# Scan decays of a hybrid encoder layer: biases inside the exponentials, feature decays broadcast by DMA, time steps by token

## The chip, the cores and the metric

One core of a Trainium2 chip runs the kernel. The metric is device time in microseconds, the median of several runs; lower is better. Engines are named as in the profile: PE is TensorE (matmuls; PEld its weight loads), DVE is VectorE, ACT is ScalarE, POOL is GpSimd, SP is the engine that issues most of the DMAs. Each works through its own list in order and waits for the others by semaphores.

## The reference, cut to what matters

The layer is a mixer of two branches (a bidirectional state space scan and windowed attention), a cross attention and a feed forward part, all in float32, with 512 tokens of 1024 features. The change concerns the scan: 32 heads of 64 features in 4 groups, 4 chunks of 128 tokens, once forward and once backward.

```python
dtf = softplus(dt_f + dt_bias_f); dtb = softplus(dt_b + dt_bias_b)   # (tokens, heads)
af = -exp(a_log_f); ab = -exp(a_log_b)                              # (heads)
def ssd_chunked(xh, dt, a_head, b_in, c_in):
    a_cum = cumsum(dt * a_head)                  # within each chunk of 128 tokens
    x_c = xh * dt
    seg = a_cum[l] - a_cum[s]
    decay = exp(where(lower, seg, -inf))         # per head and chunk, 128 x 128
    cb = einsum('bclgn,bcsgn->bclsg', c_c, b_c)  # per group
    y_diag = einsum('bclsg,bclsgr,bcsgrp->bclgrp', cb, decay, x_c)
    to_end = exp(a_cum[last] - a_cum)
    states = einsum('bclgn,bclgr,bclgrp->bcgrpn', b_c, to_end, x_c)
    chunk_decay = exp(a_cum[last])
    h_in = scan over chunks: state * chunk_decay + states
    y_off = einsum('bclgn,bcgrpn,bclgr->bclgrp', c_c, h_in, exp(a_cum))
    return y_diag + y_off
y = ssd_chunked(forward) + flip(ssd_chunked(backward)) + d_skip * xh
```

## The kernel before, in words

**Weights.** All projections run with features on the partitions and 512 tokens along the free axis. A weight granule of 128x1024 is loaded by SP (line 120) into one of two raw buffers, cast by ACT to a high part (line 128), and DVE (POOL for ten of them) subtracts to get the low part (line 129). A projection is then 24 matmuls of 512 columns, eight each of lines 138, 139 and 140. Granules are loaded and split two ahead of their use.

**Order.** The program is a list of steps, in which scan steps and projections are woven (`weave`, the strings `ONE`, `TWO`, `LAST`). A scheduler of the tile framework turns it into one order for each engine, taking what is ready by its own model of time; it also sets all waits. Tiles rotate: a tile with `bufs=2` may be written again when all readers of the tile two before are done.

**Time steps** (`dt_step`). One granule gives 64 rows (32 heads, two directions) by 512 tokens. Lines 345 to 362 compute the softplus on 64x512: ACT takes exp(-|v|), DVE evaluates a polynomial as seven pairs of a multiplication (line 354) and an addition (line 355), divides (line 349), multiplies by the head's rate (line 361); ACT takes the logarithm (line 363). PE then turns three results to tokens on partitions (`tok`, line 368, four transposes each). Matmuls with triangles give the cumulative sums, by heads (line 380) and by tokens (line 387). The rows by heads are stored to DRAM (`adr`, line 383). `nb` is log(dt) minus the cumulative sum, `wt` and `dec` are the weights of a chunk and its decay. The buffer `x1` is free then and holds what lies between. In program order the first group's convolutions follow (lines 408 to 414: one step of ACT, four of DVE, tanh on ACT, one of DVE, for each of six granules); DVE gets them mixed with the time steps.

**A group's scan** (`group_scan`). `weigh` (POOL, line 492) and `carry` (PE line 500, DVE 505 and 507) compute the states. Each of eight heads then goes through stages: `rows` loads the cumulative sums of both directions, broadcast over 128 partitions, into `rt` (line 516, three buffers); `head` lets ACT write exp of half of the partitions to `ear` (line 528: the decay by features, one tile of two buffers for a pair of heads), POOL mask both directions (line 530), ACT take the exponential of the forward part with `nb` as a bias per partition, chunk by chunk (line 536), DVE add `nb` to the backward part chunk by chunk (line 538) and ACT take the exponential of that as one instruction (line 539). `both` (POOL, line 545) adds the directions into `mt` (three buffers), `times` (DVE, line 550) multiplies by the group's `cb`, `inner` and `arrive` (PE, lines 560 and 572) are the products for a pair of heads. `gather` (lines 580 to 585) multiplies what arrives by `ear` on DVE and adds it on DVE and POOL; `gate` follows. Between the stages the next group's convolutions, the gates `z` and the former group's output projections run. At a group's end, PE turns the last convolution's output to tokens (line 467).

Of the kernel before, what the change touches and what calls it, by code (L numbers as in the profile page):

```python
# [15 lines left out]
P = 128  # L16
# [13 lines left out]
# columns of the packed constants  # L30
# [7 lines left out]
V_DTB, V_AL, V_DSK, V_SNK = 200, 201, 202, 218  # L38
V_N = 234
# granules of the input projection  # L40
# [32 lines left out]
def bidir_hybrid_layer(ctx: ExitStack, tc: tile.TileContext, io, dbg=None):  # L73
# [17 lines left out]
    adr = dram.tile([64, S], F32, tag="adr", name="adr")  # L91

# [94 lines left out]
    def gain_split(hi, lo, t, g):  # L187
        """hi + lo = t * g, exactly split."""
# [26 lines left out]
    # ======================= keys and values of the memory =======================  # L215
    # (in buffers that the state space branch uses later)
# [111 lines left out]
    # ======================= state space branch =======================  # L328
# [7 lines left out]
    # time steps: softplus, cumulative sums within chunks, decays  # L336
    # (x1 is free until the first group is projected: it holds the intermediate values)
    def dt_step(w):
        acc = proj(w, st["hh"], st["hl"])
        v, e, den, s2, pl = (x1[0:64, i] for i in range(5))  # L340

        def t256(i, o):
            return x1[:, i, 256 * o:256 * o + 256].rearrange("p (c e) -> p c e", c=NCH)
# [13 lines left out]
        dt, dta, ld = den, s2, e  # L357
        nc.vector.scalar_tensor_tensor(dt, v, 0.0, pl, op0=ALU.max, op1=ALU.add)
        an = st["sp"].tile([64, 1], F32, tag="an", name="an")
        nc.scalar.activation(an, vec[0:64, V_AL:V_AL + 1], AF.Exp)  # L360
# [860 lines left out]
```

## Time and profile before

| what | value |
|---|---|
| median of 3 runs | 1351.72 us (1351.01 to 1351.82) |
| profiled execution, from first to last instruction | 1350.6 us |
| PE, DVE, ACT, POOL busy | 1284.6, 812.4, 580.8, 316.5 us |
| time steps and first convolutions | 55 to 104 us |
| scan of four groups | 104 to 530 us |
| attention, merge, cross attention, feed forward | 530 us to the end |

Busy time of an engine is the time in which at least one instruction of it runs. Matmuls are pipelined, so PE can be busy without being at its peak. A wait names the instruction that came last among those waited for. The chain of waits is followed back from the last instruction, at each step to what released it, or to the instruction before it on its engine. The granted clock is given as a share of TensorE's full speed, averaged over the stretch.

### The profile page before, as it was taken

To read this page: it belongs to the slowest core of one execution; us is meant where nothing else is said; L and a number is where in the kernel's file an instruction comes from. 1 tells how busy PE (TensorE), PEld (TensorE's weight loads), DVE (VectorE), ACT (ScalarE), POOL (GpSimd) and SP (SyncE) were. 2 spreads that over 40 slices of the span, in tenths; PEclk is the share of its full clock that TensorE was granted. 3 is DMA by queue.
4 is the path that set the end of the run, shared out by engine and by line. 5 is a ranking of instruction groups with operands and counts; after the bars stand their busy time and mean duration, and the time that the engine had idled before them with its cause. 6 is when DMAs were issued, how large, how long until landed. Compare 5 with 4: busy or idle time off the path is not lost.

```text
span 1350.6 us, 16359 instructions
## 1 busy us (share of the span) xinstructions
PE 1284.6 (95%) x6084; PEld 1022.9 (76%) x6084; DVE 812.4 (60%) x1355; ACT 580.8 (43%) x1001; POOL 316.5 (23%) x259
## 2 busy tenths in 40 slices
PE   6889998998999999999999999999999999999996
PEld 5667776776777678876656888888888888888886
DVE  5797788788679776577765444566443444333323
ACT  6437376257256253256855333444332332222221
POOL 3344254234453562320000001100211111110001
PEclk9999999998999999999999999999999999999998
DMA  7435344243223323321102332411323322233331
GB/s 244 129 102 160 112 143 129 74 125 125 69 94 119 109 74 99 115 80 46 47 16 85 118 94 94 156 63 49 101 88 105 96 94 94 96 102 90 99 98 63
DMA packets 45440, 134.95 MB, mean 100 GB/s; under 512 B 5104, under 2 KB 8560, under 8 KB 45360
## 3 DMA queue, kind: packets, MB, share of 16 engines
q1 hardware_dynamic: 43072, 129.77, 30.4%
q10 hardware_dynamic: 1584, 2.03, 0.5%
q0 software_dynamic: 704, 2.10, 0.4%
q8 instruction: 48, 0.79, 0.2%
q14 instruction: 32, 0.26, 0.1%
HBM read 129.55 MB, written 4.33 MB: 99 GB/s over the span
## 4 chain that ended last, share of the span: by engine, by line
PE 69%; DVE 12%; issue 6%; POOL 6%; ACT 4%; DMA 2%; SPq 0%; DVEq 0%; POOLq 0%; ACTq 0%
PE mm L138 19%; PE mm L140 19%; PE mm L139 19%; DVE cvu L411 2%; DVE rt L538 2%; DVE wlo L129 2%; PE sa L774 2%; PE sb L813 2%; PE sb L800 1%; POOL mt L545 1%; POOL vv L585 1%; PE sa L772 1%; PE sb L986 1%; ACT whi L128 1%; PE sb L500 1%
## 5 line engine op out<-in xcount | busy, mean ns | idle before, releaser
L138 PE MATMUL mm<-hh,whi 128*128 128x512 f32 x968 | 388.4, 401 | 8.8 <-DVE cvu L411 5.4
L128 ACT CAST whi<-raw 128x1024 fp32r<-128x1024 f32 (+2 forms) x192 | 199.0, 1037 | 454.4 <-PE mm L139 394.0
L140 PE MATMUL mm<-hh,wlo 128*128 128x512 f32 x968 | 383.5, 397 | 0.9 <-DVE wlo L129 0.8
L139 PE MATMUL mm<-hl,whi 128*128 128x512 f32 x968 | 382.5, 395 | 0.2 <-DVE hl L310 0.2
L129 DVE TENSOR_TENSOR wlo<-raw,whi 128x1024 fp32r<-128x1024 f32 (+2 forms) x193 | 242.4, 1257 | 127.4 <-ACT whi L128 121.1
L138 PEld LDWEIGHTS mm<-hh,whi 128*128 128x128 f32 x968 | 184.8, 191 | 52.1 <-issue 10.3
L140 PEld LDWEIGHTS mm<-hh,wlo 128*128 128x128 f32 x968 | 184.2, 190 | 43.1 <-issue 2.3
L139 PEld LDWEIGHTS mm<-hl,whi 128*128 128x128 f32 x968 | 184.5, 191 | 39.0 <-issue 1.6
L185 POOL TENSOR_TENSOR sq_acc<-sq_acc,sq 128x512 f32<-128x512 f32 x14 | 24.8, 1771 | 276.4 <-ACT sq L184 276.4
L1039 POOL TENSOR_TENSOR fa<-fa,row 128x512 f32<-128x512 f32 x22 | 39.1, 1779 | 192.3 <-ACT fa L1038 192.3
L411 DVE SCALAR_TENSOR_TENSOR cvu<-mm,hcw,cvu 128x510 f32<-128x510 f32 (+1 forms) x96 | 70.9, 739 | 5.9 <-ACT cvu L408 5.5
L138 PE MATMUL mm<-fh,whi 128*128 128x512 f32 (+1 forms) x198 | 72.4, 366 | 0.0
L139 PE MATMUL mm<-fl,whi 128*128 128x512 f32 (+1 forms) x198 | 72.4, 365 | 0.0
L140 PE MATMUL mm<-fh,wlo 128*128 128x512 f32 (+1 forms) x198 | 72.4, 365 | 0.0
L138 PE MATMUL mm<-vh,whi 128*128 128x512 f32 (+1 forms) x192 | 71.5, 373 | 0.0
L140 PE MATMUL mm<-vh,wlo 128*128 128x512 f32 (+1 forms) x192 | 69.3, 361 | 0.0
L139 PE MATMUL mm<-vl,whi 128*128 128x512 f32 (+1 forms) x192 | 68.8, 358 | 0.0
L538 DVE TENSOR_SCALAR rt<-rt,nb 128x128 f32<-128x128 f32 x128 | 52.5, 466 | 20.9 <-POOL rt L530 17.5
L545 POOL TENSOR_TENSOR mt<-rt 128x512 f32<-128x512 f32 x32 | 48.0, 1503 | 71.8 <-ACT rt L539 33.8
L1041 DVE TENSOR_TENSOR ft<-fa,mm 128x512 f32<-128x512 f32 x22 | 15.1, 688 | 72.8 <-PE mm L140 70.7
L528 ACT ACTIVATE ear<-rt 64x1024 f32<-64x1024 f32 x32 | 33.9, 1060 | 55.7 <-POOL vv L585 51.9
L140 PE MATMUL mm<-oh,wlo 128*128 128x512 f32 x128 | 50.2, 392 | 0.0
(233 smaller groups left out, 2070.3 us busy)
## 6 DMA issues: line engine op xcount, KB each, us to landing
raw<-in_w_in SPq DMA_DIRECT2D x69, 512.0 KB, 3.5
raw<-in_w_fi SPq DMA_DIRECT2D x44, 512.0 KB, 3.5
rt<-adr SPq DMA_DIRECT2D x64, 256.0 KB, 4.3
raw<-in_w_bs SPq DMA_DIRECT2D x16, 512.0 KB, 3.4
raw<-in_w_fo SPq DMA_DIRECT2D x16, 512.0 KB, 3.5
raw<-in_w_xk SPq DMA_DIRECT2D x8, 512.0 KB, 3.8
raw<-in_w_ba SPq DMA_DIRECT2D x8, 512.0 KB, 3.4
raw<-in_w_mo SPq DMA_DIRECT2D x8, 512.0 KB, 3.5
```

What stands on the lines that cost most here:

```text
L128: nc.scalar.copy(hi[:, t], raw[:, t])
L129: (nc.gpsimd if i in LO_POOL else nc.vector).tensor_tensor(lo[:, t], raw[:, t], hi[:, t].bitcast(F32), op=ALU.subtract)
L138: nc.tensor.matmul(acc, wh, xh[:, k0 + k], start=first and k == 0, stop=False)
L139: nc.tensor.matmul(acc, wh, xl[:, k0 + k], start=False, stop=False)
L140: nc.tensor.matmul(acc, wl, xh[:, k0 + k], start=False, stop=last and k == nk - 1)
L411: nc.vector.scalar_tensor_tensor(u[:, b], acc[:, a], w5[j], u[:, b], op0=ALU.mult, op1=ALU.add)
L528: nc.scalar.activation(st["ear", h // 2][own], rt[own], AF.Exp)
L538: nc.vector.tensor_scalar(r, r, st["nb"][:, c, e0:e0 + 1], None, op0=ALU.add)
L545: nc.gpsimd.tensor_tensor(mt, st["rt", g, h][:, 0], st["rt", g, h][:, 1], op=ALU.add)
L774: nc.tensor.matmul(sp[:, :n], qs[own, qb * P:(qb + 1) * P], st["kl"][own, pr, b0 * P:b1 * P], start=False, stop=True)
L813: nc.tensor.matmul(av[64 * kk:64 * kk + 64], st["vt"][:, b0 + j, h * 64:(h + 1) * 64], st["pt", kk, j], start=j == 0, stop=j == b1 - b0 - 1)
L1039: nc.gpsimd.tensor_tensor(a, a, st["row2"], op=ALU.mult)
```

## The change

1. The backward part of a head gets its `nb` as a bias of four exponentials, as the forward part did: DVE's additions of line 538 and the single exponential of line 539 go.
2. The exponential of the cumulative sums is taken once for all heads on 64x512 in `dt_step`, stored to DRAM (`edr`) and broadcast by SP into `ear`, two copies of 64 partitions for a pair of heads (`earows`). The first two pairs' copies stand after the heads of steps 2 and 4, the others after the `gather` that frees their buffer. The rows of a head come as one copy of 512 KB in place of two.
3. The time steps are turned to tokens before the softplus, with four transposes, and run on 128x256; multiplications and additions are fused; the logarithm comes last. `V_AL` holds the rates broadcast over the partitions, and the vectors are 297 columns wide in place of 234.

```diff
     def dt_step(w):
         acc = proj(w, st["hh"], st["hl"])
-        v, e, den, s2, pl = (x1[0:64, i] for i in range(5))
-        nc.scalar.activation(v, acc[0:64], AF.Identity, bias=vec[0:64, V_DTB:V_DTB + 1])
-        nc.scalar.activation(e, v, AF.Abs)
+        v, e, den, s2, pl, dta, ld, acm = (slot(i) for i in range(8))
+        raw, rows, erows = (x1[0:64, i] for i in (5, 6, 7))
+        nc.scalar.activation(raw, acc[0:64], AF.Identity, bias=vec[0:64, V_DTB:V_DTB + 1])
+        tp = bank("sb")
+        tpv = tp[:, 0:256].rearrange("p (c e) -> p c e", c=NCH)
+        for c in range(NCH):
+            nc.tensor.transpose(tpv[:, c], raw[:, c * P:(c + 1) * P], ident[0:64, 0:64])
+        an = st["sp"].tile([P, 64], F32, tag="an", name="an")
+        nc.scalar.activation(an, vec[:, V_AL:V_AL + 64], AF.Exp)
+        nc.scalar.activation(e, tpv, AF.Abs)
+        nc.vector.tensor_copy(v, tpv)
         nc.scalar.activation(e, e, AF.Exp, scale=-1.0)
...
-        nc.vector.tensor_scalar(pl, s2, 2.0 / 17.0, 2.0 / 15.0, op0=ALU.mult, op1=ALU.add)
-        for n in (13, 11, 9, 7, 5, 3, 1):
-            nc.vector.tensor_tensor(pl, pl, s2, op=ALU.mult)
-            nc.vector.tensor_scalar(pl, pl, 2.0 / n, None, op0=ALU.add)
-        nc.vector.tensor_tensor(pl, pl, e, op=ALU.mult)
+        nc.vector.tensor_scalar(pl, s2, 2.0 / 17.0, None, op0=ALU.mult)
+        for n in (15, 13, 11, 9, 7, 5, 3):
+            nc.vector.scalar_tensor_tensor(pl, pl, 2.0 / n, s2, op0=ALU.add, op1=ALU.mult)
+        nc.vector.scalar_tensor_tensor(pl, pl, 2.0, e, op0=ALU.add, op1=ALU.mult)
...
-        nc.vector.tensor_scalar(dta, dt, an, -1.0, op0=ALU.mult, op1=ALU.mult)
+        anb = an.rearrange("p (o e) -> p o e", o=1).broadcast_to([P, NCH, 64])
+        nc.vector.scalar_tensor_tensor(dta, dt, -1.0, anb, op0=ALU.mult, op1=ALU.mult)
         nc.vector.tensor_scalar(ld, dt, 1e-37, None, op0=ALU.max)
-        nc.scalar.activation(ld, ld, AF.Ln)
...
-        dat = tok(dta, t256(5, 0))
-        dtt = tok(dt, t256(5, 1))
-        ldt = tok(ld, t256(7, 1))
...
-        nc.scalar.copy(x1[0:64, 6], fm[0:64])
-        nc.sync.dma_start(adr, x1[0:64, 6])
...
+        nc.vector.tensor_copy(rows, fm[0:64])
+        nc.sync.dma_start(adr, rows)
+        nc.scalar.activation(erows, rows, AF.Exp)
+        nc.sync.dma_start(edr, erows)
         nc.scalar.copy(acm, tv)
         nc.scalar.activation(dec, ov, AF.Exp)
-        nc.vector.tensor_tensor(nb, ldt, acm, op=ALU.subtract)
         nc.vector.tensor_tensor(wt, ov, acm, op=ALU.subtract)
         nc.scalar.activation(wt, wt, AF.Exp)
-        nc.vector.tensor_tensor(wt, wt, dtt, op=ALU.mult)
+        nc.vector.tensor_tensor(wt, wt, dt, op=ALU.mult)
+        nc.scalar.activation(ld, ld, AF.Ln)
+        nc.vector.tensor_tensor(nb, ld, acm, op=ALU.subtract)
...
         def rows(h):
             rt = st["sp"].tile([P, 2, S], F32, tag="rt", name="rt", bufs=RB)
             e0 = 8 * g + h
-            for d in range(2):
-                nc.sync.dma_start(rt[:, d], adr[32 * d + e0:32 * d + e0 + 1, :].broadcast_to([P, S]))
+            nc.sync.dma_start(rt, adr.rearrange("(d e) s -> e d s", d=2)[e0:e0 + 1].broadcast_to([P, 2, S]))
             st["rt", g, h] = rt
+        def earows(i):
+            def f():
+                st["ear", i] = ear = st["sp"].tile([P, 2, S], F32, tag="ear", name="ear", bufs=2)
+                for k in range(2):
+                    e0 = 8 * g + 2 * i + k
+                    nc.sync.dma_start(ear[64 * k:64 * k + 64], edr.rearrange("(d e) s -> e d s", d=2)[e0:e0 + 1]
+                                      .broadcast_to([64, 2, S]))
+            return f
         def head(h):
...
-                if h % 2 == 0:
-                    st["ear", h // 2] = sp.tile([P, 2, S], F32, tag="ear", name="ear", bufs=2)
-                own = slice(64 * (h % 2), 64 * (h % 2) + 64)
-                nc.scalar.activation(st["ear", h // 2][own], rt[own], AF.Exp)
...
-                for c in range(NCH):
-                    r, e0 = rt[:, 0, c * P:(c + 1) * P], 8 * g + h
-                    nc.scalar.activation(r, r, AF.Exp, bias=st["nb"][:, c, e0:e0 + 1])
-                    r, e0 = rt[:, 1, c * P:(c + 1) * P], e0 + 32
-                    nc.vector.tensor_scalar(r, r, st["nb"][:, c, e0:e0 + 1], None, op0=ALU.add)
-                nc.scalar.activation(rt[:, 1], rt[:, 1], AF.Exp)
+                for d in range(2):
+                    for c in range(NCH):
+                        r, e0 = rt[:, d, c * P:(c + 1) * P], 32 * d + 8 * g + h
+                        nc.scalar.activation(r, r, AF.Exp, bias=st["nb"][:, c, e0:e0 + 1])
...
             if t >= LAG3 + GLAG and (t - LAG3 - GLAG) % 2 == 0:
-                order.append(ga[(t - LAG3 - GLAG) // 2])
+                i = (t - LAG3 - GLAG) // 2
+                order += [ga[i]] + el[i + 2:i + 3]
+            if t in EL:
+                order.append(el[EL.index(t)])
```

## Rows read from the trace of the kernel before

**Rows 1.** The page, part 1: busy us (share) and instructions of each engine.
```profile
PE 1284.6 (95%) x6084; PEld 1022.9 (76%) x6084; DVE 812.4 (60%) x1355; ACT 580.8 (43%) x1001; POOL 316.5 (23%) x259
```

**Rows 2.** Windows by stage: us, PE, PEld, DVE, ACT, POOL busy, PEclk, DMA, GB/s.
```profile
55.00:104.00 49.00, 40.84 (x227) 34.11 (x225) 43.69 (x52) 21.95 (x31) 21.41 (x11) 0.97 0.31 98
104.00:212.00 108.00, 100.13 (x555) 82.35 (x556) 87.60 (x135) 65.72 (x115) 48.79 (x48) 0.97 0.46 139
212.00:320.00 108.00, 101.39 (x512) 80.55 (x511) 85.23 (x139) 53.99 (x93) 38.34 (x36) 0.98 0.35 107
320.00:430.00 110.00, 98.19 (x482) 77.38 (x482) 83.66 (x129) 52.96 (x93) 48.68 (x42) 0.95 0.34 104
430.00:530.00 100.00, 93.91 (x468) 73.36 (x468) 76.00 (x116) 45.46 (x78) 45.42 (x40) 0.97 0.30 93
530.00:1351.00 821.00, 808.56 (x3687) 643.40 (x3685) 401.07 (x734) 309.67 (x544) 99.55 (x65) 0.99 0.27 87
```

**Rows 3.** Windows, nine stretches with idle time: the longest, and their sum.
```profile
324.00:340.00 16.00, 10.28 (x39) 8.16 (x38) 12.44 (x20) 8.12 (x15) 3.38 (x3) 0.79 0.59 189
...
sum 80.00, PE 53.44 PEld 39.77 DVE 67.55 ACT 36.40 POOL 29.29; mean PE 5.94 PEld 4.42 DVE 7.51 ACT 4.04 POOL 3.25
```

**Rows 4.** Waits of PE: who waited for whom, us in total, times, longest.
```profile
PE sb L467 <- DVE xs L414: 18.4, 6, 5.7
PE mm L138 <- DVE cvu L411: 5.4, 3, 2.2
```

**Rows 5.** Chain of waits by line: whole span, 322 to 336 us, 55 to 104 us.
```profile
by line: PE mm L138 19.3%; PE mm L140 19.2%; PE mm L139 19.1%; issue 6.4%; DVE cvu L411 2.2%; DVE rt L538 2.0%; DVE wlo L129 1.7%; PE sa L774 1.6%; PE sb L813 1.6%; PE sb L800 1.4%; POOL mt L545 1.2%; POOL vv L585 1.1%; PE sa L772 0.9%; PE 
...
by line: DVE cvu L411 19.4%; DVE rt L538 16.7%; DVE vv L597 12.7%; issue 9.2%; DVE wlo L129 8.1%; PE sb L467 7.8%; DVE mt L550 6.9%; PE mm L138 6.1%; PE mm L139 6.1%; DVE vl L190 5.3%; DVE xs L414 4.4%; DVE sq_acc L185 4.3%; PE mm L140 3.0%
...
by line: DVE cvu L411 19.2%; DVE x L354 17.5%; DVE x L355 12.7%; DVE x L349 6.7%; DVE x L350 5.4%; DMA adr<-x 4.6%; DVE x L361 3.9%; PE sa L380 3.0%; PE sb L368 2.2%; issue 2.2%; ACT whi L128 2.1%; PE mm L138 2.1%; PE mm L139 1.7%; PE mm L1
```

**Rows 6.** Groups of instructions by line: scan heads on DVE and ACT, weight casts.
```profile
L128 ACT CAST whi<-raw 128x1024 fp32r<-128x1024 f32 (+2 forms) x192 | 199.0, 1037 | 454.4 <-PE mm L139 394.0 <-issue 42.3 <-DMA raw<-in_w_in 9.6
...
L538 DVE TENSOR_SCALAR rt<-rt,nb 128x128 f32<-128x128 f32 x128 | 52.5, 466 | 20.9 <-POOL rt L530 17.5 <-DMA raw<-in_w_in 3.4
...
L536 ACT ACTIVATE rt<-rt,nb 128x128 f32<-128x128 f32 x128 | 41.0, 392 | 0.5
...
L528 ACT ACTIVATE ear<-rt 64x1024 f32<-64x1024 f32 x32 | 33.9, 1060 | 55.7 <-POOL vv L585 51.9 <-DMA rt<-adr 3.4
...
L539 ACT ACTIVATE rt<-rt 128x512 f32<-128x512 f32 x32 | 20.0, 628 | 13.0 <-DVE rt L538 12.9
```

**Rows 7.** DMA issues, head rows: KB each, median us to landing.
```profile
rt<-adr SPq DMA_DIRECT2D x64, 256.0 KB, 4.3
```

**Rows 8.** Waits of SP's queue, 104 to 530 us.
```profile
SPq L120 <- DVE wlo L129: 247.1, 52, 14.6
SPq L516 <- POOL mt L545: 113.6, 27, 13.8
```

**Rows 9.** Groups by line on DVE, 55 to 104 us: time steps.
```profile
L354 DVE TENSOR_TENSOR x<-x 64x512 f32<-64x512 f32 x7 | 9.0, 1284 | 0.0
L355 DVE TENSOR_SCALAR x<-x 64x512 f32<-64x512 f32 x7 | 6.6, 948 | 0.0
L349 DVE RECIPROCAL x<-x 64x512 f32<-64x512 f32 x1 | 3.3, 3335 | 0.0
L350 DVE TENSOR_TENSOR x<-x 64x512 f32<-64x512 f32 x1 | 2.7, 2700 | 0.0
...
L395 DVE TENSOR_TENSOR nb<-x 128x256 f32<-128x256 f32 x1 | 0.4, 426 | 0.0
```

**Rows 10.** Lines 354 and 538: duration ns min/median/max.
```profile
L354 DVE TENSOR_TENSOR x<-x x7: 671/673/2875, 68.6 to 87.1; 64x512 f32<-64x512 f32 x7
...
L538 DVE TENSOR_SCALAR rt<-rt,nb x128: 268/278/1347, 112.3 to 499.5; 128x128 f32<-128x128 f32 x128
```

**Rows 11.** Store of the cumulative sums (tile adr): first and last start.
```profile
L383 SPq DMA_DIRECT2D adr<-x x1: 524/524/524, 101.9 to 101.9; - x1
```

More of the change, by code (lines that the diff above doesn't have):

```diff
@@ L37 @@
 V_CW, V_CB, V_SSD = 40, 160, 184
-V_DTB, V_AL, V_DSK, V_SNK = 200, 201, 202, 218
-V_N = 234
+V_DTB, V_DSK, V_SNK, V_AL = 200, 201, 217, 233
+V_N = 297
 G_DT, G_K, G_V, G_Q, G_GA, G_SSD, G_GS, G_N = 0, 1, 3, 5, 13, 21, 61, 69
@@ L63 @@
 RAWB, WB = 2, 3
+EL = (2, 4)
 def weave(a, b):
@@ L91, in bidir_hybrid_layer @@
     adr = dram.tile([64, S], F32, tag="adr", name="adr")
+    edr = dram.tile([64, S], F32, tag="edr", name="edr")
     def bank(tag):
@@ L339, in dt_step, with slot @@
         acc = proj(w, st["hh"], st["hl"])
-        v, e, den, s2, pl = (x1[0:64, i] for i in range(5))
-        def t256(i, o):
-            return x1[:, i, 256 * o:256 * o + 256].rearrange("p (c e) -> p c e", c=NCH)
-        nc.scalar.activation(v, acc[0:64], AF.Identity, bias=vec[0:64, V_DTB:V_DTB + 1])
-        nc.scalar.activation(e, v, AF.Abs)
+        def slot(i):
+            return x1[:, i // 2, 256 * (i % 2):256 * (i % 2) + 256].rearrange("p (c e) -> p c e", c=NCH)
+        v, e, den, s2, pl, dta, ld, acm = (slot(i) for i in range(8))
[9 more added lines that the diff above has]
+        nc.vector.tensor_copy(v, tpv)
         nc.scalar.activation(e, e, AF.Exp, scale=-1.0)
@@ L351, in dt_step @@
         nc.vector.tensor_tensor(s2, e, e, op=ALU.mult)
-        nc.vector.tensor_scalar(pl, s2, 2.0 / 17.0, 2.0 / 15.0, op0=ALU.mult, op1=ALU.add)
-        for n in (13, 11, 9, 7, 5, 3, 1):
-            nc.vector.tensor_tensor(pl, pl, s2, op=ALU.mult)
-            nc.vector.tensor_scalar(pl, pl, 2.0 / n, None, op0=ALU.add)
-        nc.vector.tensor_tensor(pl, pl, e, op=ALU.mult)
-        dt, dta, ld = den, s2, e
+        nc.vector.tensor_scalar(pl, s2, 2.0 / 17.0, None, op0=ALU.mult)
+        for n in (15, 13, 11, 9, 7, 5, 3):
+            nc.vector.scalar_tensor_tensor(pl, pl, 2.0 / n, s2, op0=ALU.add, op1=ALU.mult)
+        nc.vector.scalar_tensor_tensor(pl, pl, 2.0, e, op0=ALU.add, op1=ALU.mult)
+        dt = den
         nc.vector.scalar_tensor_tensor(dt, v, 0.0, pl, op0=ALU.max, op1=ALU.add)
-        an = st["sp"].tile([64, 1], F32, tag="an", name="an")
-        nc.scalar.activation(an, vec[0:64, V_AL:V_AL + 1], AF.Exp)
-        nc.vector.tensor_scalar(dta, dt, an, -1.0, op0=ALU.mult, op1=ALU.mult)
+        anb = an.rearrange("p (o e) -> p o e", o=1).broadcast_to([P, NCH, 64])
+        nc.vector.scalar_tensor_tensor(dta, dt, -1.0, anb, op0=ALU.mult, op1=ALU.mult)
         nc.vector.tensor_scalar(ld, dt, 1e-37, None, op0=ALU.max)
-        nc.scalar.activation(ld, ld, AF.Ln)
-        def tok(src, o):
-            b = bank("sb")
-            for c in range(NCH):
-                nc.tensor.transpose(b[:, c * 64:(c + 1) * 64], src[:, c * P:(c + 1) * P], ident[0:64, 0:64])
-            nc.scalar.copy(o, b[:, 0:256].rearrange("p (c e) -> p c e", c=NCH))
-            return o
-        dat = tok(dta, t256(5, 0))
-        dtt = tok(dt, t256(5, 1))
-        ldt = tok(ld, t256(7, 1))
         nb, wt, dec = (st[n] for n in ("nb", "wt", "dec"))
@@ L386, in dt_step @@
         for d in range(2):
-            nc.tensor.matmul(tv[:, :, 32 * d:32 * d + 32], tri[d], dat[:, :, 32 * d:32 * d + 32],
+            nc.tensor.matmul(tv[:, :, 32 * d:32 * d + 32], tri[d], dta[:, :, 32 * d:32 * d + 32],
                              start=True, stop=True)
@@ L390, in dt_step @@
         ov = tot[:, 0:256].rearrange("p (c e) -> p c e", c=NCH)
-        nc.tensor.matmul(ov, ones, dat, start=True, stop=True)
-        acm = t256(4, 0)
+        nc.tensor.matmul(ov, ones, dta, start=True, stop=True)
+        nc.vector.tensor_copy(rows, fm[0:64])
+        nc.sync.dma_start(adr, rows)
+        nc.scalar.activation(erows, rows, AF.Exp)
+        nc.sync.dma_start(edr, erows)
         nc.scalar.copy(acm, tv)
         nc.scalar.activation(dec, ov, AF.Exp)
-        nc.vector.tensor_tensor(nb, ldt, acm, op=ALU.subtract)
         nc.vector.tensor_tensor(wt, ov, acm, op=ALU.subtract)
         nc.scalar.activation(wt, wt, AF.Exp)
-        nc.vector.tensor_tensor(wt, wt, dtt, op=ALU.mult)
+        nc.vector.tensor_tensor(wt, wt, dt, op=ALU.mult)
+        nc.scalar.activation(ld, ld, AF.Ln)
+        nc.vector.tensor_tensor(nb, ld, acm, op=ALU.subtract)
         dump("dt", dt)
@@ L605, in group_scan @@
         hd, bo, ti = ([w(h) for h in range(HPG)] for w in (head, both, times))
-        nn, ar, ga, gs = ([w(i) for i in range(4)] for w in (inner, arrive, gather, gate))
+        nn, ar, ga, gs, el = ([w(i) for i in range(4)] for w in (inner, arrive, gather, gate, earows))
         order = []
@@ L1184, in layout @@
     vecs[32:64, V_DTB] = a["dt_bias_bwd"][0]
-    vecs[0:32, V_AL] = a["a_log_fwd"][0]
-    vecs[32:64, V_AL] = a["a_log_bwd"][0]
+    vecs[:, V_AL:V_AL + 32] = a["a_log_fwd"][0][None]
+    vecs[:, V_AL + 32:V_AL + 64] = a["a_log_bwd"][0][None]
     vecs[:, V_DSK:V_DSK + 16] = _cols(np.repeat(a["d_skip"][0], 64))
```

4 lines of the change are left out of this document (1 added, 3 removed).

## The prediction, made before the kernel was run

> **What bounds the kernel now.** First the engines' busy times: TensorE is busy for 1284.6 of 1350.6 us [rows 1], so nothing is gained except where it stands idle or runs at its low clock. The windows by stage show where: each row gives length, then busy time of PE, its weight loads, DVE, ACT and POOL, then the granted clock. From 530 us on, TensorE loses 12.4 of 821 us, and the change touches nothing there. Between 55 and 104 us (time steps, first convolutions) it is idle for 49 - 40.84 = 8.2 us, and the clock of 0.97 (a mixture of 2.4 and 1.2 GHz) costs another 49 x 0.03 = 1.5. In the four scan windows it is idle for 7.87 + 6.61 + 11.81 + 6.09 = 32.4 us, and the clocks of 0.97, 0.98, 0.95 and 0.97 cost 108 x 0.03 + 108 x 0.02 + 110 x 0.05 + 100 x 0.03 = 13.9 us: 46.3 in all [rows 2].
>
> Then I cut out the nine stretches where the idle time sits. Their 80 us hold 80 - 53.44 = 26.6 of the 32.4 us, and DVE is busy for 67.55 of those 80; in the longest, TensorE does 10.28 us of work in 16 and the clock falls to 0.79 [rows 3]. The waits name the same engine: 18.4 us for the last convolution's output, 5.4 for a convolution that still reads its bank [rows 4]. DVE's time there is a backlog. The chain of waits confirms it: across the gap at 322 to 336 us DVE instructions hold most of it, the bias add of line 538 alone 16.7%, and from 55 to 104 us it runs along the time-step arithmetic (lines 349 to 361) mixed with convolutions [rows 5]. So DVE, in order and nearly full, sets when TensorE can go on at the group boundaries.
>
> **Part 1, biases into the exponentials.** The 128 adds of line 538 go: 52.5 us of DVE [rows 6], out of 87.60 + 85.23 + 83.66 + 76.00 = 332.5 in the scan windows [rows 2]. ACT loses the 32 wide exponentials (20.0 us) and gets 128 more narrow ones, at the 41.0 us of the existing 128 [rows 6]. Along a head, four narrow ones then a wide one (41.0/32 + 0.63 = 1.91 us, with the adds beside) become eight narrow ones, 2.56.
>
> **Part 2, feature decays once, by DMA.** ACT's 32 exponentials of 64x1024 go: 33.9 us, and with them 51.9 us of waits, because each needs a buffer that GpSimd's gather two pairs earlier still reads; the masks, casts and convolution steps queue behind that on ACT [rows 6]. ACT's balance is +41.0 - 20.0 - 33.9 = -12.9 us, and a head's path on ACT is 0.65 longer by part 1 and 1.06 shorter here. The Trainium skill (ScalarE: Activation LUTs, Rules for kernel authors) says to use VectorE, not ScalarE, for adding; by it part 1 alone would be a loss on ACT. The rows put the sum at -12.9 with part 2 beside it, so I keep that.
>
> In return SP issues 32 copies of 512 KB and 32 of 256 KB where it issued 64 of 256 KB: as many issues, 8 MB more traffic. A 256 KB broadcast lands in 4.3 us [rows 7]. The new one writes 64 partitions with two rows each, a shape the trace does not show; bounds are 4.3 us and, if half the partitions mean half the rate, twice that. It is asked for four of a group's fourteen steps before its use, some 30 of the 108 us, so either end is hidden, and I take nothing. One exponential of 64x512 and one store are added in the time steps, off the way to the head rows, since the store of the plain rows goes first.
>
> The feature copies wait for the gather's release, now on SP: behind them stand weight loads and head rows, for which ACT's casts and GpSimd's masks wait. SP already waits 27 times, 113.6 us (mean 4.2), for head buffers, and reaches a weight load on average 247.1/52 = 4.75 us before its buffer is free [rows 8]. The eight new waits (two per group; the first two of a group find free buffers) fit under that at the mean: nothing, if the cover holds. The price without it is the slow rival.
>
> **Part 3, time steps by token.** The work goes from 64x512 to 128x256 and product and add are fused. Of the chain's costly rows, 9.0 + 6.6 + 3.3 + 2.7 us = 21.6 go [rows 9]. In their place come eight fused steps, a division and a multiplication at 256 columns: 9 x 0.43 by the 128x256 row, and half of 3.3 for the division: 5.5 us. Two new copies from PSUM cost about 0.4 and 0.7 by the same widths. That saves 21.6 - 5.5 - 1.1 = 15 us of DVE; if the fused steps are held up as the old multiplications were (the seven took 9.0 us where 7 x 0.67 = 4.7 would do [rows 9, 10]), 5.5 doubles and 9.5 is left. Four transposes before the chain replace twelve after it. The logarithm leaves the path to the store of the cumulative sums. That store starts at 101.9 us now [rows 11]; I expect 81 to 87, earlier by the 15 us and by the part of the way behind the chain (three copies and the transposes) that goes. But TensorE has its own work then: at most the 8.2 + 1.5 = 9.7 us lost there can come back. I take 6, between 0 and 9.7, since the convolutions' own DVE work stays.
>
> **Sum.** For parts 1 and 2 the ends are 0 and 46.3 us. Line 538 holds 2.0% of the chain of the whole span, 27 us [rows 5]. The adds leave nothing in their place on DVE, and the head path on ACT gets no longer, so most of the 27 should go; the backlog that ends TensorE's waits shrinks one for one. I take 25. With 6 that is 31 us: 1350.6 - 31 = 1319.6 in the profiled execution. The median of the runs, 1351.7, lies 1.1 above its span, which gives **1321 us**.
>
> **The rivals.** *The waits move on.* An add takes 268 ns at the least, 278 in the middle, 1347 at most [rows 10], and its mean spacing of 0.41 us (52.5/128) is about twice the least time a run of such instructions could need; much of the 52.5 us is therefore standing still, up to some 26. The SBUF page (SBUF — State Buffer, Who interferes with whom) says that a DVE instruction with two SBUF inputs, or in a two-port mode, and a GpSimd instruction shut each other out for a whole instruction. By that rule the standing still passes to the next such DVE instruction (products, splits), though not to convolution steps, which read PSUM. If all of it passes on, relief is 26 us in place of 52: 12 in the scan and 4 before it, 16 us, **1336**. For it: 268 against 1347 ns. Against it: in the gap the next instructions are mostly convolution steps.
>
> *TensorE becomes the bound.* All 9.7 + 46.3 = 56 us come back: **1296**. For it: DVE drops from 0.78 of the scan windows to about 0.66. Against it: waits for GpSimd and for the start of a group stay.
>
> *The same gap with another name.* ACT's eight exponentials in a row hold casts and masks up, and the gain goes into new waits: **1351**. Against it: the cast waits 394.0 us for TensorE [rows 6], so it has slack nearly everywhere.
>
> *Slower: SP stands behind a feature copy.* In each group the copies of the third and fourth pair wait on SP for the gather, with a weight load behind them. Eight waits, each longer than the slack of 4.75 us by x, cost 8x us of TensorE. From x = 3.9 (a wait of 8.6 us) it eats the 31 us. At a wait of 10 us it is 42, **1363**; at the longest wait that SP has for a head buffer, 13.8 us [rows 8], it is 72. For it: SP is in order and the loads share it. Against it: the mean there is 4.2 us, and casts wait for a weight transfer for just 9.6 us in the whole kernel [rows 6].
>
> **How the numbers follow.** Forecast 0.55; waits move on 0.22; TensorE bound 0.10; same gap 0.05; SP blocked 0.08. Faster by over 0.2% (2.7 us, about what this measurement can tell): 0.55 + 0.22 + 0.10 = 0.87; within 0.05; slower 0.08. The range of 1297 to 1343 holds the first two cases whole and much of the third, and leaves out the last two.
>
> **What would show it.** Right: DVE in the four scan windows falls by 26 to 52 us; no DVE add reads the head rows; ACT has no wait for the gather; the store of the cumulative sums starts by 87 us; the wait of the transposes for the last convolution (18.4 us) falls below 8; the windows after the scan are as before. Wrong: waits of SP for the gather beyond 9 us with casts waiting for weights; or the nine gaps of the same size with ACT or GpSimd as their last releaser; or products and splits on DVE that get longer by what the adds lost.

## The result, and the profile after

The changed kernel takes 1336.44 us (median of 4 runs, 1334.19 to 1338.11) beside 1351.37 us for the kernel before on the same chip: 14.9 us less, a ratio of 0.9887 with an interval of 0.9874 to 0.990. The gain is clear of the noise and the time inside the range of 1297 to 1343, but 15 us above the forecast of 1321: half of the expected gain is missing. All ratios below are against the kernel before, run beside each kernel on its chip.

The page of the changed kernel, engines' busy time. Its profiled execution was the fastest of the four runs; its span is 18.2 us shorter than that of before.

```profile
PE 1274.2 (96%) x6076; PEld 1017.2 (76%) x6076; DVE 774.4 (58%) x1222; ACT 565.3 (42%) x1062; POOL 319.5 (24%) x259
```

Windows by stage of the changed kernel, the columns of [rows 2].

```profile
55.00:104.00 49.00, 40.38 (x211) 33.79 (x211) 37.89 (x48) 26.95 (x51) 26.41 (x18) 0.90 0.50 146
104.00:212.00 108.00, 101.81 (x572) 84.30 (x571) 79.12 (x102) 63.37 (x143) 48.15 (x49) 0.98 0.52 158
212.00:320.00 108.00, 102.92 (x516) 82.12 (x515) 82.24 (x108) 52.80 (x113) 40.73 (x36) 0.97 0.43 130
320.00:430.00 110.00, 101.09 (x508) 80.59 (x507) 79.99 (x103) 51.72 (x111) 53.98 (x44) 0.95 0.41 123
430.00:530.00 100.00, 96.26 (x493) 76.21 (x492) 68.71 (x87) 32.27 (x53) 43.51 (x35) 1.00 0.32 101
530.00:1333.00 803.00, 790.46 (x3622) 628.85 (x3620) 391.49 (x723) 306.04 (x540) 92.28 (x61) 1.00 0.27 87
```

Against [rows 2], DVE in the four scan windows falls from 332.5 to 310.1 us, by 22.4. These windows are fixed in time, and the changed kernel does more of its program in them; over the whole kernel DVE's busy time falls by 38.0 us (812.4 to 774.4). TensorE stands idle there for 6.19 + 5.08 + 8.91 + 3.74 = 23.9 us in place of 32.4. After 530 us it loses 803 - 790.46 = 12.5 us, as before (12.4). Between 55 and 104 us it is idle for 8.6 us, no less than before (8.2), and the clock there is 0.90 in place of 0.97.

Waits of the changed kernel from 55 to 530 us, by engine (who waited for whom: us, times, longest). Lines have moved: 465 are the transposes for the last convolution, 412 its last step on DVE, 539 the exponentials of a head, 532 its masks, 513 the row copies, 522 the feature copies, 545 the sum of both directions, 585 the gather.

```profile
PE sb L465 <- DVE xs L412: 20.0, 5, 8.0
...
ACT rt L539 <- POOL rt L532: 76.8, 19, 10.1
...
POOL rt L532 <- DMA rt<-adr: 54.1, 18, 7.5
...
SPq L522 <- POOL vv L585: 58.7, 12, 9.4
SPq L513 <- POOL mt L545: 49.7, 22, 6.6
```

TensorE's wait for the last convolution did not fall: 20.0 us, against 18.4 in [rows 4]. ACT's 51.9 us of waits for the gather [rows 6] are gone, and in their place it waits 76.8 us for masks, which wait 54.1 us for the rows' DMA. One of the gaps, from the timeline of the changed kernel (start, us, engine, line, operation, count; in brackets the idle time before and what ended it):

```profile
394.83 0.39 SPq L513 DMA_DIRECT2D rt<-adr  x1
...
400.17 1.22 POOL L532 TENSOR_SCALAR_AFFINE_SELECT rt<-rt 128x512 f32<-128x512 f32 x2 [3.13 <-DMA rt<-adr]
...
400.83 0.98 ACT L539 ACTIVATE rt<-rt,nb 128x128 f32<-128x128 f32 x3 [5.57 <-POOL rt L532]
401.72 1.03 ACT L130 CAST whi<-raw 128x1024 fp32r<-128x1024 f32 x1
402.66 0.63 ACT L411 ACTIVATE cvt<-cvu 128x512 f32<-128x512 f32 x1
...
403.93 1.12 DVE L412 SCALAR_TENSOR_TENSOR xs<-cvt,cvu 128x512 f32<-128x512 f32 x1
...
405.10 1.12 PE L465 MATMUL sb<-cst,xs 128*128 128x128 f32 x4 [8.04 <-DVE xs L412]
...
408.26 2.97 POOL L545 TENSOR_TENSOR mt<-rt 128x512 f32<-128x512 f32 x2 [0.60 <-PE sa L560]
```

Read it from top to bottom: a row copy goes out, the mask starts when it has landed, ACT's exponentials wait 5.57 us for the mask, and the weight cast, the tanh of the last convolution (line 411), DVE's last step and the transposes come in a row behind them. TensorE idles for 8.04 us behind a head that it does not need yet: the sum of that head's two directions is the second of the two in the last line, over 4 us after its exponentials have ended. The wait's last releaser is named DVE, but DVE had itself just been waiting for ACT. The chain of waits of the changed kernel, by line, from 388 to 408 us, puts the row copy first, where [rows 5] had convolution steps and the add of line 538:

```profile
by line: DMA rt<-adr 26.1%; PE sa L560 9.5%; issue 8.8%; POOL rt L532 8.7%; POOL sq_acc L187 8.5%; POOL mt L545 6.3%; DVE wlo L131 6.1%; PE sb L465 5.6%; DVE xs L412 5.2%; ACT whi L130 4.7%; POOL x L643 4.6%; ACT rt L539 3.6%; DVE cvt L642
```

### The profile page after: what moved, and what is told of

Same layout as the page of the kernel before. It is cut to its first block, busy times and chain, and to the rows that moved or that the text cites. A ratio compares the mean times of both kernels' runs of the same rounds, so it can differ in the third digit from the quotient of the medians.

```text
span 1332.4 us, 16231 instructions
## 1 busy us (share of the span) xinstructions
PE 1274.2 (96%) x6076; PEld 1017.2 (76%) x6076; DVE 774.4 (58%) x1222; ACT 565.3 (42%) x1062; POOL 319.5 (24%) x259
## 4 chain that ended last, share of the span: by engine, by line
PE 72%; POOL 4%; DVE 3%; DMA 3%; issue 2%; ACT 1%; SPq 0%; DVEq 0%; POOLq 0%; ACTq 0%
PE mm L140 21%; PE mm L142 21%; PE mm L141 20%; DMA rt<-adr 2%; PE sb L816 2%; PE sa L777 2%; PE sb L803 1%; PE sb L989 1%; PE sa L775 1%; POOL mt L545 1%; PE sa L958 1%; PE sa L560 1%; DVE wlo L131 1%; DMA raw<-in_w_in 1%; POOL xw L490 1%
## 5 line engine op out<-in xcount | busy, mean ns | idle before, releaser
L539 ACT ACTIVATE rt<-rt,nb 128x128 f32<-128x128 f32 x256 | 79.5, 392 | 76.9 <-POOL rt L532 76.8
L140 PE MATMUL mm<-fh,whi 128*128 128x512 f32 (+1 forms) x198 | 72.4, 366 | 0.0
L141 PE MATMUL mm<-fl,whi 128*128 128x512 f32 (+1 forms) x198 | 72.4, 365 | 0.0
L142 PE MATMUL mm<-fh,wlo 128*128 128x512 f32 (+1 forms) x198 | 72.4, 365 | 0.0
L532 POOL TENSOR_SCALAR_AFFINE_SELECT rt<-rt 128x512 f32<-128x512 f32 x64 | 51.5, 827 | 54.7 <-DMA rt<-adr 54.1
```

The costliest lines, as they stand in the source:

```text
L140: nc.tensor.matmul(acc, wh, xh[:, k0 + k], start=first and k == 0, stop=False)
L141: nc.tensor.matmul(acc, wh, xl[:, k0 + k], start=False, stop=False)
L142: nc.tensor.matmul(acc, wl, xh[:, k0 + k], start=False, stop=last and k == nk - 1)
L532: nc.gpsimd.affine_select(out=rt[:, d].rearrange("p (c l) -> p c l", c=NCH), in_=rt[:, d].rearrange("p (c l) -> p c l", c=NCH), pattern=[[ ...
L539: nc.scalar.activation(r, r, AF.Exp, bias=st["nb"][:, c, e0:e0 + 1])
```

## Experiments: each part alone

Part 1 alone: the kernel before with all eight exponentials narrow and biased.

```diff
-                    nc.vector.tensor_scalar(r, r, st["nb"][:, c, e0:e0 + 1], None, op0=ALU.add)
-                nc.scalar.activation(rt[:, 1], rt[:, 1], AF.Exp)
+                for d in range(2):
...
+                        nc.scalar.activation(r, r, AF.Exp, bias=st["nb"][:, c, e0:e0 + 1])
```

> The kernel before with part 1 alone (the biases inside the exponentials); feature decays still taken by ACT in every head, time steps as before. Three theories. DVE RELIEF: the adds were what TensorE waited for, so most of the 15 us gained by the whole change comes with them: 1340 to 1343. LOCK: some 20 of the 52 us only pass to other DVE instructions that read two SBUF tiles, so it gives 5 to 8 us: 1343 to 1346. ACT ORDER: the narrow exponentials stand in ACT's order before casts and tanh and wait for the masks, while the feature exponentials with their wait for the gather are still there; ACT is 21 us busier: 1348 to 1356.

Measured: 1331.29 us (1329.07 to 1334.54), ratio 0.9858 (0.9838 to 0.9877), 19.5 us less than the 1350.79 beside it. This one part gains more than the whole change. Its engines' busy time, its scan windows and the wait of the transposes:

```profile
PE 1273.2 (96%) x6084; PEld 1014.9 (76%) x6084; DVE 777.9 (59%) x1227; ACT 598.8 (45%) x1097; POOL 320.3 (24%) x259
...
104.00:212.00 108.00, 103.52 (x589) 85.48 (x588) 80.37 (x106) 78.23 (x158) 51.62 (x50) 1.00 0.51 149
212.00:320.00 108.00, 102.42 (x525) 81.55 (x524) 83.75 (x110) 63.11 (x128) 41.55 (x37) 1.00 0.39 115
320.00:430.00 110.00, 101.42 (x520) 80.74 (x521) 79.72 (x106) 62.15 (x125) 52.53 (x45) 0.99 0.37 109
430.00:530.00 100.00, 97.95 (x488) 76.93 (x487) 68.44 (x85) 38.42 (x70) 49.82 (x41) 0.99 0.28 89
...
PE sb L467 <- DVE xs L414: 8.6, 6, 2.4
```

In these windows DVE falls by 20.2 us (332.5 to 312.3), but they hold more of the program than before (2122 matmuls in place of 2017). Over the whole kernel DVE's busy time falls by 34.5 us (812.4 to 777.9), and the time by 19.5. TensorE's idle time in the windows goes from 32.4 to 20.7 us, and the clock from 0.97, 0.98, 0.95, 0.97 to 1.00, 1.00, 0.99, 0.99. With the longest wait of the transposes down from 5.7 to 2.4 us, the granted clock stays at or near the upper of its two levels (2.4 GHz), and the 13.9 us of clock loss become 2.1, reckoned as in the prediction.

Part 2 alone: the kernel before with feature decays by DMA and a head's rows as one copy.

```diff
-                nc.scalar.activation(st["ear", h // 2][own], rt[own], AF.Exp)
...
+                    nc.sync.dma_start(ear[64 * k:64 * k + 64], edr.rearrange("(d e) s -> e d s", d=2)[e0:e0 + 1]
+                                      .broadcast_to([64, 2, S]))
```

> The kernel before with part 2 alone (feature decays once, by DMA; rows of a head in one copy). DVE RELIEF: DVE keeps all its adds, so little changes: 1347 to 1352. LOCK: the same, 1347 to 1352. ACT ORDER: the 33.9 us of feature exponentials and their 51.9 us of waits for the gather leave ACT's order, so more than half of the gain is here: 1340 to 1344.

Measured: 1362.39 us (1355.94 to 1364.95), ratio 1.0081 (1.0052 to 1.011): 11.6 us more. Alone, part 2 makes the kernel slower. ACT waits 72.1 us for masks and GpSimd 72.4 us for rows, and the transposes wait 25.0 us for the last convolution (here lines 544, 538 and 471):

```profile
POOL rt L538 <- DMA rt<-adr: 72.4, 21, 11.2
ACT rt L544 <- POOL rt L538: 72.1, 20, 10.6
...
PE sb L471 <- DVE xs L418: 25.0, 5, 10.1
```

The picture of the changed kernel is that of part 2.

Part 3 alone: the kernel before with the new `dt_step`, without the store of `edr`.

```diff
-        nc.vector.tensor_scalar(pl, s2, 2.0 / 17.0, 2.0 / 15.0, op0=ALU.mult, op1=ALU.add)
...
+            nc.vector.scalar_tensor_tensor(pl, pl, 2.0 / n, s2, op0=ALU.add, op1=ALU.mult)
...
```

> The kernel before with part 3 alone (time steps by token). All theories: the store of the cumulative sums starts near 82 us instead of 102, but TensorE stands for the first triangle matmuls as it does in the whole change, and the convolutions' DVE work stays: 1347 to 1351. If the forecast of 6 us held, 1345.

Measured: 1342.37 us (1339.92 to 1344.11), ratio 0.9936 (0.9919 to 0.9954): 8.4 us less. The gain does not lie where the time steps run. Windows of this kernel:

```profile
55.00:104.00 49.00, 41.19 (x227) 34.94 (x227) 39.98 (x60) 27.84 (x45) 26.31 (x18) 0.93 0.43 131
104.00:150.00 46.00, 45.68 (x236) 36.44 (x235) 32.58 (x47) 21.25 (x33) 13.15 (x13) 1.00 0.39 130
```

The second window in the kernel before:

```profile
104.00:150.00 46.00, 40.91 (x187) 31.21 (x188) 33.86 (x49) 26.92 (x48) 18.55 (x18) 0.96 0.48 139
```

From 55 to 104 us TensorE does as many matmuls as before (227) and is idle for 7.8 us in place of 8.2, at a clock of 0.93 in place of 0.97. From 104 to 150 us, at the start of the scan, it is idle for 0.3 us in place of 5.1, at a clock of 1.00 in place of 0.96; the first product of a head (line 550 before) starts at 95.4 us in place of 123.6.

And the changed kernel with the old time steps, parts 1 and 2 alone:

```diff
-            nc.vector.scalar_tensor_tensor(pl, pl, 2.0 / n, s2, op0=ALU.add, op1=ALU.mult)
...
+            nc.vector.tensor_tensor(pl, pl, s2, op=ALU.mult)
+            nc.vector.tensor_scalar(pl, pl, 2.0 / n, None, op0=ALU.add)
...
```

> The change without part 3 (old time steps, with the exponential of the sums and its store added). If part 3 gives nothing by itself: 1336 to 1338, as the whole change. If the forecast of 6 us for it held: 1342. LOCK and ACT ORDER both say 1336 to 1340.

Measured: 1343.61 us (1343.12 to 1347.55), ratio 0.9954 (0.9939 to 0.997), 7.2 us less than before. So part 3 is worth 0.0067 of the time, 9 us, in the whole, as alone; and part 2 on top of part 1 costs 0.9954 - 0.9858 = 0.0096, 13 us.

Parts 1 and 3, the changed kernel without part 2 (and, in the first of two, with a head's rows as two copies again):

```diff
-                    nc.sync.dma_start(ear[64 * k:64 * k + 64], edr.rearrange("(d e) s -> e d s", d=2)[e0:e0 + 1]
...
+                nc.scalar.activation(st["ear", h // 2][own], rt[own], AF.Exp)
```

> The change without part 2 (ACT takes the feature decays in every head, rows of a head in two copies). If part 2 is what gives back, as the run of part 2 alone says (+11.6), and parts 1 and 3 add (-19.5 and -8.4): 1323, faster than the whole change by 13. If part 2 only cost in company with the DVE adds: 1334 to 1338.

Measured: 1327.22 us (1326.11 to 1329.08), ratio 0.9828 (0.9814 to 0.9843): 23.9 us less than the 1351.16 beside it. The second keeps the one copy of 512 KB:

```diff
-            for d in range(2):
-                nc.sync.dma_start(rt[:, d], adr[32 * d + e0:32 * d + e0 + 1, :].broadcast_to([P, S]))
+            nc.sync.dma_start(rt, adr.rearrange("(d e) s -> e d s", d=2)[e0:e0 + 1].broadcast_to([P, 2, S]))
```

> The change without part 2, but with the rows of a head in one copy of 512 KB. COPY SIZE: the mask of the first direction waits for 5.9 us instead of 4.3, and this alone gives back most of part 2's loss: 8 us or more above the version with two copies. SP ORDER: the loss is from the feature copies that hold SP's queue, and this is within 2 us of the version with two copies.

Measured: 1325.28 us (1323.51 to 1327.98), ratio 0.9808 (0.9792 to 0.9825). The larger copy costs nothing here; with part 2, two copies were not tried. Waits of this kernel (lines 461 and 408 are the transposes and the last convolution, 521 the old wide exponential, 576 the gather), and what idle time ahead of its head rows the copies ended:

```profile
PE sb L461 <- DVE xs L408: 7.9, 6, 3.1
...
ACT ear L521 <- POOL vv L576: 34.3, 9, 8.2
...
  DMA rt<-adr: 4.6, 3
```

With the old exponentials in place, ACT waits for the gather again, 34.3 us, and this does no harm; rows are waited for during 4.6 us in place of 54.1, and the transposes' wait is 7.9 us, under the 8 that was asked of the change. Part 2 costs 8 us (0.9887 - 0.9828) to 11 us (0.9887 - 0.9808) of what parts 1 and 3 bring.

## Experiments: what in part 2 costs it

First, SP's order: the feature copies wait on SP for the gather (58.7 us), with row copies behind them. One run leaves half of these copies out, and one gives them to GpSimd's queue.

```diff
+                if i >= 2:
+                    st["ear", i] = st["ear", i - 2]
+                    return
```

> The whole change, with the copies of the feature decays left out for the third and fourth pair of each group, whose gather reads what the first two pairs left in the two buffers. SP ORDER: the copies that wait on SP for the gather are gone, so the head rows behind them come in time: 1322 to 1328. COPY SIZE: 1334 to 1338, as the whole change.

Measured: 1337.65 us (1336.74 to 1339.93), ratio 0.9907 (0.9892 to 0.9922): no better than the changed kernel. SP's waits for the gather fell to 32.3 us, and ACT's waits for masks rose to 91.6.

```diff
-                    nc.sync.dma_start(ear[64 * k:64 * k + 64], edr.rearrange("(d e) s -> e d s", d=2)[e0:e0 + 1]
+                    nc.gpsimd.dma_start(ear[64 * k:64 * k + 64], edr.rearrange("(d e) s -> e d s", d=2)[e0:e0 + 1]
```

> The whole change, with the feature copies issued by GpSimd, which runs the gather's last addition itself, in place of SP. SP ORDER: SP's queue is free of the waits for the gather: 1323 to 1330, less GpSimd's own time for 32 issues of some 0.6 us, part of it on the masks' way. COPY SIZE: 1336 to 1342.

Measured: 1342.83 us (1341.2 to 1345.56), ratio 0.9945 (0.9927 to 0.9962), slower than the changed kernel. SP had no wait for the gather left, and ACT and GpSimd waited as before:

```profile
ACT rt L539 <- POOL rt L532: 77.7, 19, 10.2
...
POOL rt L532 <- DMA rt<-adr: 57.5, 23, 5.9
```

SP's order is not the main cause. The changed kernel's own trace agrees: 22 of the 29 row copies that take a used buffer start within 0.2 us of the end of the sum that frees it. Second, pace: the old wide exponential waited for the gather, and so perhaps kept ACT from running ahead to a head whose rows had not come. This run gives ACT a copy of one column that waits as the old exponential did.

```diff
+                    nc.scalar.copy(st["pace", h // 2], rt[:, 0, 0:1])
...
+                nc.gpsimd.tensor_tensor(st["pace", i], st["pace", i], vv[:, 0:1], op=ALU.add)
```

> The whole change, with one column of a pair's first rows copied by ACT, before the mask, into a tile of two buffers that the gather releases at its end: the wait for the gather that the old feature exponentials had, without their work. PACE: without that wait ACT comes to a head's exponentials before the rows have landed and stands there with casts and tanh behind it; with it ACT does these first, and the time falls to 1318 to 1327, the waits of ACT for the masks (76.8 us) below 35. LATENCY: rows come as late as before and the wait is only one more: 1336 to 1345.

Measured: 1372.01 us (1371.69 to 1372.65), ratio 1.0156 (1.0141 to 1.0171). The wait was there (25.7 us on ACT), but the waits for masks rose to 97.8. A wait of that kind, added, does not bring the time back: the kernel is slower than before. It does not bring back the old order of the work either, as the last rows of this section show.

Third, the exponentials stand in program order right behind the masks; here they stand one step of the program later.

```diff
-            for w, lag in ((hd, 0), (bo, LAG1), (ti, LAG2)):
+            for w, lag in ((hd, 0), (xo, LAG1), (bo, LAG1), (ti, LAG2)):
```

> The whole change, with the exponentials of a head one step of the program later than its masks, so that casts and tanh of the step between come before them. PACE: 1322 to 1330, waits of ACT for the masks below 45 us. LATENCY: the chain of a head is as long as before and the next rows' buffer comes free later: 1336 to 1345.

Measured: 1339.04 us (1332.35 to 1340.9), ratio 0.9902 (0.9867 to 0.9937), not told apart from the changed kernel. ACT still waits 71.1 us for masks: the scheduler makes its own order of ACT's list, and a step in the program moves little in it.

Fourth, room for rows: four row buffers in place of three, with `ear` in one buffer to make space.

```diff
-RB = 3
+RB = 4
...
-                st["ear", i] = ear = st["sp"].tile([P, 2, S], F32, tag="ear", name="ear", bufs=2)
+                st["ear", i] = ear = st["sp"].tile([P, 2, S], F32, tag="ear", name="ear", bufs=1)
```

> The whole change, with four buffers for the rows of a head in place of three and one for the feature decays in place of two (each pair's copies then wait for the gather just before). PACE: rows land before ACT asks for them: waits of GpSimd for the rows (54.1 us) below 20, time 1323 to 1331. If the one buffer of the feature decays holds the gather up instead: 1336 to 1345.

Measured: 1330.88 us (1329.96 to 1332.8), ratio 0.9853 (0.9837 to 0.9869): about 5 us (0.0034) better than the changed kernel, half of what part 2 costs. But the waits did not go as expected:

```profile
PE sb L465 <- DVE xs L412: 14.6, 6, 6.1
...
ACT rt L539 <- POOL rt L532: 63.7, 14, 9.5
...
POOL rt L532 <- DMA rt<-adr: 52.9, 17, 5.7
```

GpSimd's waits for rows stay at 52.9 us; only the longest shrink, 7.5 to 5.7. What gained the 5 us is not shown; the transposes' wait is 5.4 us shorter.

Why the waits for rows stay is seen when the same head is followed in the kernel without part 2 and with one row copy: the third head of the last group, the one of the gap above. Its copy is the second of the two (384.38 us); lines 523 and 530 are masks and exponentials, 536 the sum of both directions.

```profile
382.31 2.45 SPq L509 DMA_DIRECT2D rt<-adr  x2
...
410.35 1.05 ACT L521 ACTIVATE ear<-rt 64x1024 f32<-64x1024 f32 x1
...
412.39 2.12 POOL L523 TENSOR_SCALAR_AFFINE_SELECT rt<-rt 128x512 f32<-128x512 f32 x2
...
416.24 2.45 ACT L530 ACTIVATE rt<-rt,nb 128x128 f32<-128x128 f32 x8
...
418.83 1.29 POOL L536 TENSOR_TENSOR mt<-rt 128x512 f32<-128x512 f32 x1 [4.32 <-issue]
```

Here the rows land at 389.7 us and lie in their buffer for 20 us; then ACT's feature exponential, masks, exponentials and sum follow each other closely. In the changed kernel the mask starts as the rows land, and the finished exponentials lie there until the sum. The starts and landings in the traces show the same over the 32 heads of every kernel. In the six kernels where ACT takes the feature decays, the first reader starts 14.1 to 14.4 us after its rows have landed (median of a kernel's heads), and the sum 0.1 us after the last exponential. In the eight kernels with part 2 the mask starts 0.1 us after the landing (1.2 in the run with the added wait), and the sum 10 to 14 us after the last exponential; with four buffers it is 31. So the longer waits with part 2 come less from late rows than from early readers: the scheduler puts a head's masks and exponentials right behind the filling of its buffer, well before its sum, and ACT and GpSimd wait out the copy of rows that are not needed yet. A fourth buffer only lets a head be taken up earlier still.

## Experiment: VectorE and GpSimd in the time steps

Nine granules have their low part subtracted by GpSimd (not ten, as the description of the kernel and the expectation below have it), and most of these fall into the time steps and first convolutions. Here DVE does them all, on top of parts 1 and 3 and one row copy.

```diff
-LO_POOL = range(10, 19)
+LO_POOL = range(0, 0)
```

> The run without part 2 and with one row copy (1325.28 us), with the ten subtractions of low parts that GpSimd does given to VectorE too; nothing is left out. In that run the eight of them between 50 and 120 us take GpSimd 19.1 us (2391 ns each), and the seven fused time steps beside them 7.2 us (mean 1034 ns, least 409). HELD theory (VectorE's time steps are held up by these subtractions, whole instructions at a time): the fused steps fall to their least time, 7 x 0.41 = 2.9 us, and the reciprocal and the square beside them below 1 us each; VectorE gains ten subtractions of 1.23 us = 12 us and loses at least 4.4 + 2.5 = 7 us of standing still, so the time stays within 3 us of 1325. Rival, BACKLOG (the time steps are not held by GpSimd, the longest ones are something else): the fused steps keep a mean near 1000 ns, VectorE's 12 us come on top in a stretch where TensorE stands idle 6.8 of 49 us, and the time goes up by 5 to 12 us, to 1330 to 1337.

Measured: 1317.94 us (1317.36 to 1319.43), ratio 0.9762 (0.9746 to 0.9779), 32.1 us less than the 1350.08 beside it: the fastest of all kernels here. The fused time steps (duration ns: least, middle, most) and the window from 55 to 104 us, without part 2 and with one row copy:

```profile
L362 DVE SCALAR_TENSOR_TENSOR x<-x x7: 407/425/2602, 66.4 to 75.0; 128x256 f32<-128x256 f32 x7
...
55.00:104.00 49.00, 42.24 (x233) 35.90 (x233) 38.38 (x51) 29.56 (x53) 26.45 (x19) 0.93 0.46 132
```

The same kernel with all low parts on DVE:

```profile
L362 DVE SCALAR_TENSOR_TENSOR x<-x x7: 410/411/415, 62.5 to 69.5; 128x256 f32<-128x256 f32 x7
...
55.00:104.00 49.00, 47.36 (x261) 40.03 (x261) 42.08 (x65) 32.53 (x57) 9.64 (x11) 1.00 0.50 161
```

Not one fused step is held up any more, at the same operands and size; the longest falls from 2602 to 415 ns. DVE does 14 instructions more in the window, most of them subtractions of 1.2 us, for 3.7 us more busy time. TensorE's loss there goes from 6.8 us idle plus 49 x 0.07 = 3.4 of clock to 1.6 us. This run, and not part 3, gets back what the prediction saw lost in this window. HELD's mechanism is what the rows show (except that the reciprocal keeps its 1.74 us, which is its own time), but the gain of 6 us (0.9808 - 0.9762 = 0.0046) is more than either theory gave. The run does not split it between the lifted hold and the low parts themselves, which took GpSimd 2433 ns each and take DVE 1215.

## Why the prediction came out as it did, point by point

**The step that failed is part 2 costed as a relief.** The prediction counted ACT's 33.9 us of exponentials and 51.9 us of waits as gone, checked the DMA side for size and for SP's waits, and wrote "I take nothing". Measured, part 2 costs 11.6 us alone and 8 to 13 us beside the other parts; parts 1 and 2 together, taken as 25 us, bring 7.2. The relief of ACT was real (565.3 us busy, no wait for the gather), but the prediction took the order of the work as given. With the feature exponential gone nothing holds a head's masks back but its rows, the scheduler puts them right behind the landing, and ACT, which is in order, stands 76.8 us for masks with casts and the tanh of the convolutions behind. The copy of a head's rows, 4.3 us in [rows 7] and 5.9 now, had been hidden; it came to lie on the way.

**Part 1** was right in direction and too large in size: 19.5 us alone, where line 538 held 27 us of the chain [rows 5]. That the backlog "shrinks one for one" did not hold: of the 52.5 us of the adds DVE's busy time loses 34.5 in the run of part 1 alone, and the time 19.5. The other 18 us went in good part where the rival *waits move on* said: to other DVE instructions with two inputs in SBUF. Groups by line of before (products of line 550, last convolution steps of line 414):

```profile
L550 DVE TENSOR_TENSOR mt<-mt,cb 128x512 f32<-128x512 f32 x32 | 22.1, 697 | 12.0 <-POOL mt L545 12.0
...
L414 DVE SCALAR_TENSOR_TENSOR xs<-cvt,cvu 128x512 f32<-128x512 f32 x16 | 10.9, 681 | 0.1
```

The same groups of the changed kernel:

```profile
L550 DVE TENSOR_TENSOR mt<-mt,cb 128x512 f32<-128x512 f32 x32 | 32.7, 1038 | 12.8 <-POOL mt L545 12.8
...
L412 DVE SCALAR_TENSOR_TENSOR xs<-cvt,cvu 128x512 f32<-128x512 f32 x16 | 17.5, 1093 | 9.7 <-ACT cvt L411 9.7
```

In the changed kernel these two take back 10.6 + 6.6 = 17.2 us; in the run of part 1 alone it is less, 861 and 813 ns each, some 7 us. So the rival's 1336, the time that came, was reached by luck: DVE's relief was 34.5 us and not 26, part 1 gained 19.5 us in the scan and not 12, and part 2, at which this rival put no cost, made up the difference.

The Trainium skill (SBUF — State Buffer, Who interferes with whom) says that a DVE instruction with two SBUF inputs contends with a GpSimd instruction that reads SBUF, and that the port pair they share is an exclusive lock. The last run agrees: the fused steps take 2602 ns at most with GpSimd's subtractions beside them, 415 without. The Trainium skill (ScalarE: Activation LUTs, Rules for kernel authors) says to use VectorE and not ScalarE for an add. For an add that rides as the bias of an exponential, the measurement decides otherwise: in the run of part 1 alone ACT is busy 598.8 us in place of 580.8, and the time falls by 19.5.

**Part 3** was taken as 6 us and is 8.4 alone and 9 in the whole, within its bounds of 0 and 9.7, but the bound was set on the wrong stretch. The 9.7 us lost between 55 and 104 us did not come back (7.8 us idle and 49 x 0.07 = 3.4 of clock in the run of part 3 alone); the gain came behind it, from 104 to 150 us, with the heads starting earlier. The path went as forecast, with the store of the sums at 81.4 us (81 to 87 expected, 101.9 before [rows 11]). The fused steps were held up as feared: 7.2 us for the seven in the changed kernel, mean 1035 ns.

**The rivals.** *The same gap with another name* had part 2's mechanism, exponentials that hold casts up, but put the blame on their length and not on their waiting, and it priced it at the whole gain; it took 8 to 13 us. *SP behind a feature copy*: the waits came (58.7 us, 12 times where eight were counted, longest 9.4), but casts wait for weights only 10.8 us in the whole kernel in place of 9.6, and halving SP's waits or moving them away gained nothing; refuted as the main cause. *TensorE becomes the bound* did not happen: 23.9 us of idle time remain in the scan.

**What the signs said.** Right: the store, no DVE add, no wait of ACT for the gather, the windows after the scan. Wrong: DVE in the scan windows fell by 22.4 us and not 26 to 52 (38.0 over the whole kernel, whose program moves forward through the windows), the wait of the transposes stayed at 20.0, products got longer. With part 2 out and one row copy, the transposes' wait is 7.9.

**What stays open.** That part 2 costs 8 to 13 us is what the runs show. That with it heads are taken up as soon as their rows land, and that ACT and GpSimd wait there, is what the traces show, the eight kernels with part 2 against the six without. That this order is the whole cost is not shown. Each kernel gets its own order of all engines' lists from the scheduler, and an order held fixed while part 2 alone changes was not tried; nor was part 2 with a head's rows as two copies, though the larger copy's 1.6 us lie on the way of every head there. SP's waits are not the main cause, by the two runs above.

## What to carry to other kernels

Work and a wait taken off an engine that runs in order are no gain by themselves: ask what that engine reaches next, whether its inputs are there by then, and what stands behind it in its list. A wait can be what keeps a scheduler from starting work long before it is needed; when waits for a copy grow, look first whether the copy has become later or its reader earlier. And run the parts of a change singly, since here one part alone gained more than all three. Count the relief of VectorE net of what its neighbours lose to GpSimd, by comparing an instruction's least time with its mean; where the two differ by a factor, moving GpSimd's work off a stretch that is short of VectorE can pay although VectorE then does more.

## What was not expected of the hardware

The broadcast of 256 KB to 64 partitions lands as fast as the one to 128 did (4.3 us, [rows 7]); the bound of twice that, for half of the partitions, was not approached. DMA issues of the changed kernel (KB each, median us to landing):

```profile
rt<-adr SPq DMA_DIRECT2D x32, 512.0 KB, 5.9
ear<-edr SPq DMA_DIRECT2D x32, 256.0 KB, 4.4
```

And twice the bytes to 128 partitions cost 1.6 us of landing time, not double. In the run of part 1 alone, half of what the scan windows won back, 11.8 of 23.5 us, was the granted clock and not idle time. The page agrees: TensorE's busy time for the same 6084 matmuls falls by 11.4 us (1284.6 to 1273.2), its idle time over the whole span by 10.3 (66.0 to 55.7).
